# Both feed-forward products by Strassen's algorithm, in a two-block transformer kernel on one core

## The chip, the core and the metric

The kernel runs on one core of a Trainium2 chip. The metric is the device time of one execution in microseconds (us), start to end. The profile calls the engines PE (TensorE, matrix products), PEld (its weight loads), DVE (VectorE), ACT (ScalarE), POOL (GpSimd) and SP (SyncE, which here issues the DMA transfers). SBUF is the on-chip memory; the PE accumulates into PSUM, in banks of 128 x 512 fp32 numbers, which DVE or ACT read out; HBM is the memory off the core.

## What is computed

The input `x` is 1024 x 1024 in fp32. A first block (a pooling mixer and sliding attention) and the attention half of a second block come ahead of the part that matters here, the feed forward at the end. It widens 1024 features to 4096 and brings them back:

```python
def second_block(x, ...):
    ...
    x = x + merged @ w_out
    h2 = rms_norm(x, norm2)
    x = x + jnp.square(jax.nn.relu(h2 @ w_up)) @ w_down    # 1024 -> 4096 -> 1024
    return rms_norm(x, final_norm)
```

## The kernel before, in words

Tiles are 128 partitions x 512 fp32 numbers (256 KB) and come from one pool of slots; a slot is free again when its last reader is done. Nothing is multiplied in fp32 directly: each operand is split into a rounded part `h` and a rest `l = x - h`, and each product of two 128-deep slices is made by three matmuls, h times h, h times l and l times h, into one PSUM bank. ACT makes the `h` (line L106, CAST). The `l` is a subtraction on line L109: weights (`wl`) on POOL, activations (`hl`, `fl`) on DVE. Line L96 holds every matmul, L101 every transpose on the PE, L140 the weight loads by DMA.

The program is written out without hardware loops, and each engine executes its own list in order. An emitter sets that order: `e.at(dt, f)` puts an operation into its engine's list when the PE's emitted work has gone on by `dt` ns, `e.need(key)` forces what a matmul needs into the lists ahead of it, and `interleave(a, b, ...)` mixes two such pieces. These dt only decide the order; waiting is done by semaphores.

The feed forward has eight rounds `c`. Each makes 512 hidden features (function `g_T` with `up_evac`): 4 groups x 2 halves of the rows x 8 slices x 3 = 192 matmuls of 512 columns, result transposed. ACT takes the bank by a relu (L1397), DVE squares (L1399), ACT and DVE split (L106, L109). Then `down(c)` adds that round's part of the second product to the residual, which stays in SBUF: 8 row tiles x 2 halves x 4 slices x 3 = 192 matmuls, each bank added by one DVE operation (L1424). The last round's `down_last` also squares for the final norm (L380) and scales (L1452, L1453); there the last row tile's second half is made in two pieces of 256 columns. All eight rounds hold 3,072 matmuls of 512 columns' worth.

Ahead of it stands `out2(1)`, which ends the attention half: DVE evacuates (L1372), ACT squares and sums (L380), POOL forms the reciprocal root (L114, L115), DVE scales (L1380). The PE transposes the scaled rows (L101, tile `xs` to bank `tp`), ACT and DVE make the split from the bank (L392 `hh`, L396 `hl`). Those transposes are mixed between matmuls, four row tiles in `out2(1)`, the others in the first round.

## Time and profile before

| what | us |
|---|---|
| median of 3 runs (lowest, highest) | 1907.5 (1907.17, 1907.57) |
| the profiled execution's own time | 1907.2 |
| its span, first to last instruction | 1905.5 |
| PE busy in the span | 1881.4 |
| DVE, ACT, POOL busy | 904.5, 792.1, 497.0 |
| feed forward's first matmul; the last matmul's end | 1198.48; 1898.83 |

The profiled execution is 1.7 us longer than its span and 0.3 us below the median. The page of the profile gives busy time by engine and in 40 slices of the span (47.6 us each); a digit is tenths of the slice.

### The profile page before, as it was taken

What the parts mean: (1) busy time and instruction counts of PE and PEld (TensorE: products, weight loads), DVE (VectorE), ACT (ScalarE), POOL (GpSimd) and SP (SyncE); (2) the same over time, 40 slices, a digit from 0 to 9 for tenths busy, and PEclk for the clock granted to TensorE, in tenths of its full rate; (3) what the DMA queues carried; (4) which work ended last, traced back from release to release, by engine and by line L of the source; (5) the groups of instructions that cost most, each with busy time, mean ns of one, the idle gap of its engine ahead of it and who ended that gap; (6) DMA issues with size and microseconds to landing.
All of it is one profiled execution on the core that took longest, in us unless ns stands there. A gap on an engine that the chain in (4) does not pass through costs nothing.

```text
span 1905.5 us, 25049 instructions
## 1 busy us (share of the span) xinstructions
PE 1881.4 (99%) x9401; PEld 1587.8 (83%) x9401; DVE 904.5 (47%) x1841; ACT 792.1 (42%) x1677; POOL 497.0 (26%) x545
## 2 busy tenths in 40 slices
PE   7999999999999999999999999999999999999998
PEld 6888878898898888889888888888888888888887
DVE  6587882735555565665664524422232222222225
ACT  6455463537657676564553222313030212212033
POOL 4122242603312222221112322223140312213131
PEclk9999999999999999999999999999999999999999
DMA  7011132404323222111117341102111111102012
...
DMA packets 152313, 128.51 MB, mean 67 GB/s; under 512 B 12848, under 2 KB 120064, under 8 KB 152192
## 3 DMA queue, kind: packets, MB, share of 16 engines
...
q14 instruction: 47, 0.39, 0.1%
...
## 4 chain that ended last, share of the span: by engine, by line
PE 93%; DVE 3%; ACT 2%; issue 1%; POOL 1%; DMA 0%; POOLq 0%; SPq 0%; ACTq 0%; DVEq 0%
PE mm L96 56%; PE mmo L96 25%; PE tp L101 4%; PE S L96 4%; PE O L96 4%; DVE s L906 1%; ACT junk L380 0%; POOL ry L115 0%; DVE sb L641 0%; ACT sb L632 0%; DVE x L760 0%; DVE ptl L109 0%; DVE sb L626 0%; DMA x<-in_x 0%; ACT q L455 0%
## 5 line engine op out<-in xcount | busy, mean ns | idle before, releaser
L109 POOL TENSOR_TENSOR wl<-wr,wh 128x512 fp32r<-128x512 f32 x292 | 396.5, 1364 | 1104.8 <-ACT wh L106 542.7
L96 PE MATMUL mm<-hh,wh 128*128 128x512 f32 (+1 forms) x1048 | 413.7, 395 | 0.0
L96 PE MATMUL mm<-hl,wh 128*128 128x512 f32 (+1 forms) x1048 | 409.6, 391 | 1.6 <-DVE hl L791 1.6
L96 PE MATMUL mm<-hh,wl 128*128 128x512 f32 (+1 forms) x1048 | 409.0, 390 | 0.0
L96 PEld LDWEIGHTS mm<-hh,wl 128*128 128x128 f32 x1048 | 197.7, 189 | 42.4
L96 PEld LDWEIGHTS mm<-hl,wh 128*128 128x128 f32 x1048 | 198.2, 189 | 36.4 <-DVE hl L791 2.1
L96 PEld LDWEIGHTS mm<-hh,wh 128*128 128x128 f32 x1048 | 198.2, 189 | 35.2
L632 ACT ACTIVATE sb<-sb,nm 128x128 f32<-128x128 f32 (+2 forms) x192 | 125.6, 655 | 149.4 <-DVE nm L626 99.2
L1397 ACT ACTIVATE r<-mmo 128x512 f32<-128x512 f32 x32 | 19.2, 599 | 382.1 <-PE mmo L96 382.1
L106 ACT CAST wh<-wr 128x512 fp32r<-128x512 f32 x292 | 175.7, 616 | 0.7 <-DMA wr<-in_w_in 0.3
L109 DVE TENSOR_TENSOR ptl<-tp,pth 128x512 fp32r<-128x512 f32 (+2 forms) x176 | 113.5, 646 | 79.9 <-ACT pth L106 75.8
L1399 DVE TENSOR_TENSOR r<-r 128x512 f32<-128x512 f32 x64 | 44.3, 692 | 204.8 <-ACT r L1397 204.8
L106 ACT CAST pth<-tp 128x512 fp32r<-128x512 f32 (+2 forms) x176 | 96.4, 548 | 74.0 <-PE tp L101 69.8
L96 PE MATMUL mmo<-hh,wh 128*128 128x512 f32 x272 | 106.9, 393 | 0.0
L96 PE MATMUL mmo<-hh,wl 128*128 128x512 f32 x272 | 105.9, 389 | 0.0
L96 PE MATMUL mmo<-hl,wh 128*128 128x512 f32 x272 | 105.8, 389 | 0.0
L101 PE MATMUL tp<-ident,sb 128*128 128x128 f32 x648 | 99.7, 272 | 1.3 <-DVE ptl L109 1.0
L641 DVE TENSOR_SCALAR sb<-sb,rc 128x128 f32<-128x128 f32 (+2 forms) x192 | 97.6, 508 | 6.7
L96 PE MATMUL mmo<-wh,fh 128*128 128x512 f32 x260 | 100.7, 387 | 0.0
L96 PE MATMUL mmo<-wl,fh 128*128 128x512 f32 x260 | 100.7, 387 | 0.0
L96 PE MATMUL mmo<-wh,fl 128*128 128x512 f32 x260 | 100.7, 387 | 0.0
L101 PEld LDWEIGHTS tp<-ident,sb 128*128 128x128 f32 x648 | 80.5, 140 | 22.9 <-DVE ptl L109 1.8
...
## 6 DMA issues: line engine op xcount, KB each, us to landing
wr<-in_w_in SPq DMA_DIRECT2D x116, 256.0 KB, 3.4
wr<-in_w_up SPq DMA_DIRECT2D x64, 256.0 KB, 3.2
wr<-in_w_down SPq DMA_DIRECT2D x64, 256.0 KB, 3.2
wr<-in_w_out SPq DMA_DIRECT2D x32, 256.0 KB, 3.8
g_d<-g SPq DMA_DIRECT2D x32, 256.0 KB, 2.1
gl<-g_d SPq DMA_DIRECT2D x32, 256.0 KB, 5.8
...
x<-in_x SPq DMA_DIRECT2D x16, 256.0 KB, 2.9
```

The costliest lines, as they stand in the source:

```text
L96: self.nc.tensor.matmul(out=out, lhsT=lhsT, rhs=rhs, start=start, stop=stop)
L101: self.nc.tensor.transpose(out, in_, ident)
L106: self.nc.scalar.copy(out, in_)
L109: (eng or self.nc.vector).tensor_tensor(out=out, in0=in0, in1=hi.bitcast(F32), op=ALU.subtract)
L632: ACT.activation(d[:, 0:w], d[:, 0:w], AF.Exp, bias=nm, scale=-1.0, accum_out=g.sm[:, j:j + 1])
L641: V.tensor_scalar(out=d[:, 0:w], in0=d[:, 0:w], scalar1=g.rc[:, j:j + 1], scalar2=None, op0=ALU.mult)
L906: V.tensor_tensor(out=nxt[:, a0:1040], in0=cur[:, a0:1040], in1=cur[:, a0 - n:1040 - n], op=ALU.add)
L1397: ACT.activation(r0, ps, AF.Relu)
L1399: e.at(600, lambda: V.tensor_tensor(out=r1, in0=r0, in1=r0, op=ALU.mult))
```

## The change

Both products of the feed forward are done by Strassen's algorithm, in Winograd's form (7 products of half-size blocks instead of 8, with 15 sums). In the first product `q` counts 16 pairs of feature groups. Each `q` has 7 products of 4 slices x 3 matmuls = 84 matmuls of 512 columns; the sums over weight blocks (4 for each `q`, line L1491) are made on DVE from loaded tiles, and the sums over blocks of the activations once, from the transposes' banks (`prep0` L1606 to L1608, `prep1` L1625 to L1627, and L1635). Products 1 and 2 accumulate in one bank, and so do 5 and 3; a copy or a sum of the bank is taken in between (L1695, L1743, L1686), and the PE waits for it. The first three `q` go through `up_first` in another product order while the transposes of the second half are mixed in: eight transposes, twelve matmuls, eight transposes, four times. The other thirteen go through `up_pair`, with six PSUM banks in turn.

ACT makes relu and square of a hidden tile (L1660, L1661), DVE four sums of hidden tiles for each `q` (in `sums`), and the seven operands are stored to `hid_d` in HBM, 256 KB each (L1655). The residual goes to HBM too (L1420). The second product has 4 rounds `c` of 7 products x 4 row tiles x 4 slices x 3 = 336 matmuls. Each reads 28 hidden tiles back (L1540) and 16 weight tiles (L1545), makes 16 weight sums (L1491) and 56 splits: `h` on ACT (L109), `l` on POOL or, 5 of 14, on DVE (L112). DVE adds the banks to sums in SBUF (L1686; in round 0 two of the seven products are copied by ACT, L1830), 28 a round. The final norm's last piece is 512 columns wide. The feed forward has 2,688 matmuls of 512 columns. The core of the diff:

```diff
+        if self.wide:
+            pool, tag = ((self.mmp, "mm"), (self.op, "O"), (self.tp, "T"))[self.turn % 3]
+            return pool.tile([128, 512], F32, name="mm" + tag, tag=tag)
...
+    def tick(self):
+        if self.pos < min(self.goal, len(self.steps)) and self.e.t >= self.next:
+            self._one()
+            self.next = self.e.t + self.gap
+    def need(self, key, ahead):
+        i = self.mark[key]
+        while self.pos < i:
+            self._one()
+        self.goal = max(self.goal, i + ahead)
...
-    for c in range(8):
-        for f in range(4):
-            W.add(f"up{c}{f}", colunit(w_up, c * 512 + f * 128))
-        for f in range(4):
-            W.add(f"dn{c}{f}", [rowhalf(w_down, 4 * c + f, ch) for ch in range(2)])
...
+                        SY.dma_start(out=x2_d[t * 128:(t + 1) * 128, 512 * j:512 * j + 512], in_=x2.pop((t, j)))
...
+        def split(self, src, dst, last, on_dve=0):
+
+            def f():
+                r = self.raw.pop(src) if last else self.raw[src]
+                h, l = e.u(F32R, "fh"), e.u(F32R, "fl")
+                e.hi(h, r)
+                self.n_lo += 1
+                eng = V if self.n_lo * on_dve % 14 < on_dve else POOL
+                self.late.append(lambda: e.lo(l, r, h, eng))
+                self.parts[dst] = (h, l)
+            self.step(f, src, mark=dst)
...
+        def comb(self, dst, x, y, op, eng=V):
+            def f():
+                if dst not in self.raw:
+                    self.raw[dst] = e.u(name="cb")
+                eng.tensor_tensor(out=self.raw[dst], in0=self.raw[x], in1=self.raw[y], op=op)
+            self.step(f, x, y)
...
+    ORDER = (1, 2, 7, 6, 4, 5, 3)
...
+        for q in qs:
+            sp(q, "a", 1, 1), sp(q, "w", "11", 1, False)
+        for q in qs:
+            cm(q, "t3", "12", "22"), sp(q, "a", 2, 2), sp(q, "w", "21", 2, False)
+        for q in qs:
+            cm(q, "12", "12", "11"), sp(q, "a", 7, 7), cm(q, "11", "22", "12"), sp(q, "w", "t3", 7)
+        for q in qs:
+            cm(q, "21", "21", "11"), sp(q, "a", 6, 6), sp(q, "w", "11", 6)
+        for i, n in ((4, "21"), (5, "12"), (3, "22")):
+            for q in qs:
+                sp(q, "a", i, i), sp(q, "w", n, i)
...
+            ps = tr4(0, k)
+            key = ("11", k) if k < 4 else ("12", k - 4)
+            r = HR[key] = e.u(name="hr")
+            h, l = HA[key] = e.u(F32R, "hh"), e.u(F32R, "hl")
+            g = gains[:, 2, k:k + 1]
+            e.at(50, lambda ps=ps, h=h, g=g: ACT.activation(h, ps, AF.Copy, scale=g))
+            e.at(650, lambda ps=ps, r=r, g=g: ACT.activation(r, ps, AF.Copy, scale=g))
+            e.at(800, lambda ps=ps, h=h, l=l, g=g: V.scalar_tensor_tensor(
+                out=l, in0=ps, scalar=g, in1=h.bitcast(F32), op0=ALU.mult, op1=SUB), ("A", *key))
+            yield 436.0
...
+            p21, p22 = tr4(1, k), tr4(1, k + 4)
+            e.at(50, lambda p22=p22, h=h, g2=g2: ACT.activation(h, p22, AF.Copy, scale=g2))
+            e.at(50, lambda p21=p21, x21=x21, g1=g1: V.tensor_scalar(out=x21, in0=p21, scalar1=g1, scalar2=None, op0=ALU.mult))
+            e.at(800, lambda p21=p21, s3=s3, g1=g1, r11=r11: stt(s3, p21, g1, r11, SUB))
+            e.at(1500, lambda p22=p22, s1=s1, g2=g2, x21=x21: stt(s1, p22, g2, x21, ADD))
+            e.at(2200, lambda p22=p22, l=l, g2=g2, h=h: stt(l, p22, g2, h.bitcast(F32), SUB), ("A", "22", k))
+            e.at(2900, lambda p22=p22, s2=s2, g2=g2, s3=s3: stt(s2, p22, g2, s3, ADD), ("s2", k))
+            asplit("s1", k, s1, 2400, POOL)
+            asplit("s3", k, s3, 4500, POOL)
+            asplit("s2", k, s2, 5500, V)
+            e.at(12000 + 1000 * k, lambda r12=r12, s2=s2: V.tensor_tensor(out=r12, in0=r12, in1=s2, op=SUB))
+            asplit("s4", k, r12, 14000 + 1000 * k, POOL)
+            yield 872.0
...
+    def prod(ps, q, i, first=True, ahead=11):
+        wh, wl = F.take((q, i), ahead)
+        for k in range(4):
+            e.need(("A", ANAME[i], k))
+            h, l = HA[ANAME[i], k]
+            c = slice(k * 128, k * 128 + 128)
+            e.mm(ps, wh[:, c], h, first and k == 0, False, not first)
+            e.mm(ps, wh[:, c], l, False, False, not first)
+            e.mm(ps, wl[:, c], h, False, k == 3, not first)
+            yield 650.0
...
+    def sums(q):
+        h11, h12, h21, h22 = (hs.pop((q, n)) for n in ("11", "12", "21", "22"))
+        s1, s3 = e.u(name="hc"), e.u(name="hc")
+        V.tensor_tensor(out=s3, in0=h21, in1=h11, op=SUB)
+        V.tensor_tensor(out=s1, in0=h21, in1=h22, op=ADD)
+        store(q, 1, h11), store(q, 4, h22), store(q, 5, s1), store(q, 7, s3)
+        s2 = h21
+
+        def f():
+            V.tensor_tensor(out=s2, in0=h22, in1=s3, op=ADD)
+            s4 = e.u(name="hc")
+            V.tensor_tensor(out=s4, in0=h12, in1=s2, op=SUB)
+            store(q, 2, h12), store(q, 6, s2), store(q, 3, s4)
+        e.at(1800, f)
...
+        for q in qs:
+            ps = e.mmt()
+            yield from prod(ps, q, 1, True, 6)
+            e.at(50, lambda q=q, ps=ps: keep(1, q, ps), ("keep", q))
+            e.need(("keep", q))
+            yield from prod(ps, q, 2, False, 6)
+            e.at(50, lambda q=q, ps=ps: c11(q, ps))
...
+    def up_pair(q):
+        st = {}
+        X = e.mmt()
+        yield from prod(X, q, 1)
+
+        def k1():
+            st["u2"] = e.u(name="pk")
+            ACT.copy(st["u2"], X)
...
+        Y = e.mmt()
+        yield from prod(Y, q, 6)
+        e.need(("k1", q))
+        e.at(50, lambda: vadd(st["u2"], Y, st["u2"]), ("u2", q))
+        yield from prod(X, q, 2, False)
+        e.at(50, lambda: c11(q, X))
+        Z = e.mmt()
+        yield from prod(Z, q, 7)
+
+        def k3():
...
+        Vb = e.mmt()
+        yield from prod(Vb, q, 5)
+
+        def k5():
+            c = e.u(name="hc")
+            vadd(c, Vb, st["u3"])
+            relu2(c, c, q, "22")
+        e.at(50, k5, ("k5", q))
...
+        e.need(("k5", q))
+        yield from prod(Vb, q, 3, False)
...
-            for ch in range(2):
-                ps = e.mmt()
-                yield from n_group(ps, hid, t // 4, t, {f: wp[f][ch] for f in range(4)}, range(4))
-                xt = x2[t, ch]
-                e.at(50, lambda ps=ps, xt=xt: V.tensor_tensor(out=xt, in0=ps, in1=xt, op=ALU.add))
...
+    def down_prod(c, i):
+        qs = range(4 * c, 4 * c + 4)
+        F.s.gap, F.look = 800.0, 14
+        for q in qs:
+            F.s.need((q, "w", i), 14)
+        F.flush()
+        ops = [(F.parts.pop((q, "a", i)), F.parts.pop((q, "w", i))) for q in qs]
+        go_on = i in (2, 3)
+        for t in range(4):
+            tc_ = slice(t * 128, t * 128 + 128)
+            if go_on:
+                e.need(("bank", t))
+            else:
+                banks[t] = e.mmt()
+            ps = banks[t]
+            for j, ((h, l), (wh, wl)) in enumerate(ops):
+                e.mm(ps, h[:, tc_], wh, j == 0 and not go_on, False, go_on)
+                e.mm(ps, h[:, tc_], wl, False, False, go_on)
+                e.mm(ps, l[:, tc_], wh, False, j == 3, go_on)
+                yield 650.0
+            if go_on:
+                del banks[t]
+            if c == 0 and i in (1, 7):
+                g = acc[i, t] = e.u(name="acc")
+                e.at(50, lambda ps=ps, g=g: ACT.copy(g, ps), ("bank", t))
...
+            g = acc[1 if i == 6 else i, t]
+            e.at(50, lambda ps=ps, g=g: vadd(g, ps, g), ("bank", t))
...
+    for c in range(4):
+        for i in ORDER:
+            if c == 0 and i in (2, 4, 5, 3):
+                for t in range(4):
+                    x_load(i, t)
+            run(down_prod(c, i))```

Where instructions stand now shows at three places. First ACT, where the feed forward begins; `junk` is the sum of squares for the norm, `x_...` a row tile. Before, with the relu `r` of the first bank and the splits `hh` of the transposes:

```order
L392 ACTIVATE hh<-tp,gains 128x512 x3
L380 ACTIVATE junk,ss_11798<-x_12001 128x512
L380 ACTIVATE junk,ss_11831<-x_12054 128x512
L392 ACTIVATE hh<-tp,gains 128x512
L1397 ACTIVATE r<-mmo 128x512
L106 CAST fh<-r 128x512
L392 ACTIVATE hh<-tp,gains 128x512 x4
```

Of the change, with the copy `pk` of a bank after product 1 and the relu and square `hc` after product 2:

```order
L407 ACTIVATE junk,ss_11798<-x_11987 128x512
L407 ACTIVATE junk,ss_11827<-x_12053 128x512
L1695 COPY pk<-mmo 128x512
L1660 ACTIVATE hc<-mmo 128x512
L1661 ACTIVATE hc<-hc 128x512
L1626 ACTIVATE hh<-tp,gains 128x512
L1695 COPY pk<-mm 128x512
L109 CAST hh<-hr 128x512
L1626 ACTIVATE hh<-tp,gains 128x512
L109 CAST hh<-hr 128x512
L109 CAST fh<-wr 128x512
L1660 ACTIVATE hc<-mm 128x512
```

The copy is new between the two halves of one accumulation, and splits of sums (`hh<-hr`) have joined. Second DVE, at the same place. Before:

```order
L1380 TENSOR_SCALAR xs<-x_11727,ry 128x512
L1380 TENSOR_SCALAR xs<-x_12054,ry 128x512
L396 SCALAR_TENSOR_TENSOR hl<-tp,gains,hh 128x512
L1399 TENSOR_TENSOR r<-r 128x512
L109 TENSOR_TENSOR fl<-r,fh 128x512
L396 SCALAR_TENSOR_TENSOR hl<-tp,gains,hh 128x512 x4
```

Of the change:

```order
L1415 TENSOR_SCALAR xs<-x_12053,ry 128x512
L1627 TENSOR_SCALAR hr<-tp,gains 128x512
L1625 SCALAR_TENSOR_TENSOR hr<-tp,gains,hr 128x512 x2
L1625 SCALAR_TENSOR_TENSOR hl<-tp,gains,hh 128x512
L1625 SCALAR_TENSOR_TENSOR hr<-tp,gains,hr 128x512
L1627 TENSOR_SCALAR hr<-tp,gains 128x512
L1625 SCALAR_TENSOR_TENSOR hr<-tp,gains,hr 128x512 x2
L1625 SCALAR_TENSOR_TENSOR hl<-tp,gains,hh 128x512
L112 TENSOR_TENSOR hl<-hr,hh 128x512
L1625 SCALAR_TENSOR_TENSOR hr<-tp,gains,hr 128x512
```

For a pair of banks DVE had two operations (`hl`); now it has five, and from the second pair on a split of a sum (L112) among them. Third DVE in the second product, round 1, as product 2 gives way to product 7. Before, this engine's list in `down` held only the additions:

```order
L1424 TENSOR_TENSOR x_11531<-mmo,x_11531 128x512
L1424 TENSOR_TENSOR x_11832<-mm,x_11832 128x512
L1424 TENSOR_TENSOR x_11533<-mmo,x_11533 128x512
L1424 TENSOR_TENSOR x_11834<-mm,x_11834 128x512
L1424 TENSOR_TENSOR x_11547<-mmo,x_11547 128x512
```

Of the change, with the weight sums (`wr<-wr`) and the rests `fl`:

```order
L1686 TENSOR_TENSOR x_15187<-mmT,x_15187 128x512
L1491 TENSOR_TENSOR wr<-wr 128x512 x2
L112 TENSOR_TENSOR fl<-cb,fh 128x512
L1686 TENSOR_TENSOR x_15189<-mmmm,x_15189 128x512
L1491 TENSOR_TENSOR wr<-wr 128x512
L1686 TENSOR_TENSOR x_15191<-mmO,x_15191 128x512
L1491 TENSOR_TENSOR wr<-wr 128x512 x2
L112 TENSOR_TENSOR fl<-ha,fh 128x512
L1491 TENSOR_TENSOR wr<-wr 128x512
L1686 TENSOR_TENSOR x_15193<-mmT,x_15193 128x512
L1491 TENSOR_TENSOR wr<-wr 128x512
L112 TENSOR_TENSOR fl<-wr,fh 128x512
```

Weight sums and rests now stand in one list with the additions that free the banks.

## Rows read from the trace of the kernel before

**Rows 1.** The page of the profile: the span, then each engine's busy us, share and instruction count, then the busy tenths of PE in 40 slices and the TensorE clock that was granted in each.

```profile
span 1905.5 us, 25049 instructions
...
PE 1881.4 (99%) x9401; PEld 1587.8 (83%) x9401; DVE 904.5 (47%) x1841; ACT 792.1 (42%) x1677; POOL 497.0 (26%) x545
...
PE   7999999999999999999999999999999999999998
...
PEclk9999999999999999999999999999999999999999
```

**Rows 2.** Busy time in two stretches, before the feed forward and the feed forward: stretch, its us, then busy us (and instruction count) of PE, PEld, DVE, ACT, POOL, the granted clock, the DMA engines' busy share, GB/s.

```profile
0.00:1198.48 1198.48, 1181.07 (x6286) 1007.50 (x6286) 692.54 (x1548) 627.49 (x1375) 317.90 (x395) 1.00 0.27 78
1198.48:1898.83 700.35, 700.34 (x3117) 580.27 (x3115) 210.64 (x290) 163.36 (x299) 177.99 (x147) 1.00 0.16 50
```

**Rows 3.** The chain of work that ended last, three pieces in the feed forward: start, us, what, and how many instructions.

```profile
1300.27 5.44 PE mmo L96 x24
...
1675.63 5.44 PE mm L96 x24
1681.07 2.72 PE mmo L96 x12
```

**Rows 4.** PE's timeline around one group of four transposes: start, us of one, line, operation. The matmul ahead of the transposes starts at 1205.53.

```profile
1205.53 0.40 PE L96 MATMUL mm<-hh,wl 128*128 128x512 f32 x1
1205.76 0.60 PE L101 MATMUL tp<-ident,xs 128*128 128x128 f32 x4
1206.12 0.47 PE L96 MATMUL mm<-hh,wh 128*128 128x512 f32 x1
1206.43 0.39 PE L96 MATMUL mm<-hl,wh 128*128 128x512 f32 x1
```

**Rows 5.** ACT's timeline: it takes a finished bank, at the point where the first piece of [rows 3] begins.

```profile
1300.30 0.60 ACT L1397 ACTIVATE r<-mm 128x512 f32<-128x512 f32 x1 [2.88 <-PE mm L96]
```

**Rows 6.** ACT's and DVE's timelines at the entry to the feed forward: start, us, operation, idle time before it and what ended it.

```profile
1184.54 0.69 ACT L392 ACTIVATE hh<-tp,gains 128x512 fp32r<-128x512 f32 x1 [1.14 <-PE tp L101]
...
1185.26 0.75 DVE L396 SCALAR_TENSOR_TENSOR hl<-tp,gains,hh 128x512 fp32r<-128x512 f32 x1 [1.07 <-ACT hh L392]
...
1198.68 0.69 DVE L1372 SCALAR_TENSOR_TENSOR x<-mm,x 128x512 f32<-128x512 f32 x1 [1.78 <-PE mm L96]
...
1199.46 0.60 ACT L380 ACTIVATE junk<-x 128x512 f32<-128x512 f32 x1 [4.67 <-DVE x L1372]
```

**Rows 7.** Groups of instructions by line and shape from 1300 to 1800 us: operands, count | busy us, mean ns of one | idle us before them and what ended it.

```profile
L109 POOL TENSOR_TENSOR wl<-wr,wh 128x512 fp32r<-128x512 f32 x94 | 131.1, 1402 | 345.6 <-issue 212.8 <-ACT wh L106 116.4 <-DMA wr<-in_w_up 12.2
L106 ACT CAST wh<-wr 128x512 fp32r<-128x512 f32 x94 | 56.1, 615 | 0.0
L109 DVE TENSOR_TENSOR fl<-r,fh 128x512 fp32r<-128x512 f32 x47 | 42.6, 907 | 34.0 <-ACT fh L106 29.9 <-PE mmo L96 4.1
L1399 DVE TENSOR_TENSOR r<-r 128x512 f32<-128x512 f32 x47 | 32.6, 693 | 156.2 <-ACT r L1397 156.2
L1424 DVE TENSOR_TENSOR x<-mmo,x 128x512 f32<-128x512 f32 x46 | 31.8, 692 | 81.2 <-PE mmo L96 81.1
L1397 ACT ACTIVATE r<-mm 128x512 f32<-128x512 f32 x24 | 14.4, 599 | 73.3 <-PE mm L96 73.3
```

**Rows 8.** Durations of one kind of operation over the whole span, count, then ns shortest/median/longest, first and last start, and shape (first three rows); then four timeline rows of POOL and DVE, two where they overlap in time and two where they don't, start and us.

```profile
L109 POOL TENSOR_TENSOR wl<-wr,wh x292: 1277/1297/1897, 7.9 to 1846.9; 128x512 fp32r<-128x512 f32 x146
...
L109 DVE TENSOR_TENSOR fl<-r,fh x64: 691/962/1026, 1207.3 to 1857.2; 128x512 fp32r<-128x512 f32 x64
...
L1334 DVE TENSOR_TENSOR gl<-gl x16: 691/692/1306, 1027.0 to 1108.6; 128x512 f32<-128x512 f32 x16
...
1301.49 3.00 POOL L109 TENSOR_TENSOR wl<-wr,wh 128x512 fp32r<-128x512 f32 x2 [2.39 <-ACT wh L106]
...
1302.31 1.02 DVE L109 TENSOR_TENSOR fl<-r,fh 128x512 fp32r<-128x512 f32 x1 [0.69 <-ACT fh L106]
...
1329.52 0.69 DVE L109 TENSOR_TENSOR fl<-r,fh 128x512 fp32r<-128x512 f32 x1 [0.69 <-ACT fh L106]
...
1335.52 5.06 POOL L109 TENSOR_TENSOR wl<-wr,wh 128x512 fp32r<-128x512 f32 x4 [9.28 <-ACT wh L106]
```

**Rows 9.** Transfers. First a stretch with the most traffic, for the matmuls alone: stretch, its us, busy us (and count) of PE and PEld, granted clock, DMA share, GB/s; then all packets from 1198 to 1898 us; then DMA issues on SP, start, us of eight, and of one kind the count, KB each and median us from issue to landing, for a store to HBM and the load of the same data.

```profile
1025.00:1047.00 22.00, 22.00 (x99) 18.22 (x98) 1.00 1.07 351
...
DMA packets 40233, 34.82 MB, mean 50 GB/s; under 512 B 2064, under 2 KB 30736, under 8 KB 40198
...
1010.47 3.72 SPq L1281 DMA_DIRECT2D oa<-o_d  x8
...
g_d<-g SPq DMA_DIRECT2D x32, 256.0 KB, 2.1
gl<-g_d SPq DMA_DIRECT2D x32, 256.0 KB, 5.8
```

**Rows 10.** The end: DVE's and ACT's last additions and sums of squares, of 512 and of 256 columns.

```profile
1896.39 0.69 DVE L1438 TENSOR_TENSOR x<-mmo,x 128x512 f32<-128x512 f32 x1
...
1897.17 0.60 ACT L380 ACTIVATE junk<-x 128x512 f32<-128x512 f32 x1 [0.46 <-DVE x L1438]
...
1898.85 0.42 DVE L1438 TENSOR_TENSOR x<-mmo,x 128x256 f32<-128x256 f32 x1 [0.25 <-PE mmo L96]
...
1899.37 0.39 ACT L380 ACTIVATE junk<-x 128x256 f32<-128x256 f32 x1 [0.63 <-DVE x L1438]
```

More of the change, by code (lines that the diff above doesn't have):

```diff
@@ L72, in pe @@
         self.t += ns
-        if self.weights is not None:
-            self.weights.tick()
+        for w in self.streams:
+            w.tick()
         while self.heap and self.heap[0][0] <= self.t:
@@ L1360, in out2 @@
             W.want(0, base + min(5, (t + 1) // 2 + 1), base + min(4 if ch == 0 else 3, (t + 2) // 2))
+            if ch == 1 and t >= 3:
+                F.load(0, min(N0, t - 2))
+                F.ahead(6 * min(N0, t - 3))
             for k in range(8):
@@ L1365, in out2 @@
             out2_evac(ch, t, ps)
+            if t == 3 and ch == 1:
+                for k in range(8):
+                    del mT[k, 0]
     def out2_evac(ch, t, ps):
@@ new lines, in block_kernel, with asplit, tr4 @@
+    for c in range(4):
+        down_steps(c)
+    HA, HR = {}, {}
+    def asplit(key, k, r, dt, eng):
+        h, l = e.u(F32R, "hh"), e.u(F32R, "hl")
+        HA[key, k] = (h, l)
+        e.at(dt, lambda: e.hi(h, r))
+        e.at(dt + 650, lambda: e.lo(l, r, h, eng), ("A", key, k))
+    def tr4(half, k):
+        ps = e.tp.tile([128, 512], F32, name="tp", tag="T")
+        for j in range(4):
+            e.tr(ps[:, j * 128:(j + 1) * 128], xs2[4 * half + j][:, k * 128:(k + 1) * 128], ident)
+        return ps
@@ new lines, in prep0 @@
+    def prep0():
+        for t in range(4):
+            e.need(("xs2", t))
+        for k in range(KT):
+            ps = tr4(0, k)
[9 more added lines that the diff above has]
+        for t in range(4):
+            xs2.pop(t)
@@ L1458, in block_kernel @@
[L1458 to L1475 removed]
+    interleave(up_first(), prep1, lambda: xs2_t[7], 4)
@@ new lines, in gain, with last @@
+    def gain(t, ch):
+        y = e.u(name="xg")
+        V.tensor_tensor(out=y, in0=xgf[t, ch], in1=gfin[:, 512 * ch:512 * ch + 512], op=ALU.mult)
+        xgf[t, ch] = y
+    def last(row, tail=False):
+        ss, x = ssf.pop(row), [xgf.pop((row, ch)) for ch in range(2)]
+        POOL.tensor_tensor(out=ss[:, 2:3], in0=ss[:, 0:1], in1=ss[:, 1:2], op=ADD)
+        r = e.rstd(ss[:, 2:3])
+        for ch in range(2):
+            if not tail:
+                V.scalar_tensor_tensor(out=x[ch], in0=x[ch], scalar=r, in1=gfin[:, 512 * ch:512 * ch + 512],
+                                       op0=ALU.mult, op1=ALU.mult)
+            elif ch == 0:
+                V.tensor_scalar(out=x[ch], in0=x[ch], scalar1=r, scalar2=None, op0=ALU.mult)
+            else:
+                ACT.activation(x[ch], x[ch], AF.Copy, scale=r)
+            SY.dma_start(out=out_d[row * 128:(row + 1) * 128, 512 * ch:512 * ch + 512], in_=x[ch])
@@ L1476, in block_kernel @@
+    for c in range(4):
+        for i in ORDER:
+            if c == 0 and i in (2, 4, 5, 3):
+                for t in range(4):
+                    x_load(i, t)
+            run(down_prod(c, i))
     e.flush()
```

323 lines of the change are left out of this document (246 added, 77 removed).

## The prediction, made before the changed kernel had run

> **What bounds the kernel now.** I began with the page's busy times [rows 1]: PE works 1881.4 of 1905.5 us, every other engine under half, and after the first slice every digit of PE is 9 at the full clock. The two stretches [rows 2] say it more sharply for the part that changes: in the feed forward's 700.35 us PE is busy for 700.34, while DVE has 210.64, ACT 163.36, POOL 177.99. The chain of waits there [rows 3] is matmul after matmul with nothing between: 24 in 5.44 us, so 0.2267 us each. That accounts for the stretch: 3,072 x 0.2267 = 696.3, and eight groups of transposes at some 0.46 (from the matmul at 1205.53 to that at 1206.12 are 0.59 us where 0.23 would do, and the next one comes late by another 0.1 [rows 4]) are 3.7; together 700.0. So the time here is the number of matmuls, as long as the operands arrive.
>
> **The change, part by part.** The sum is made against the profiled execution, 1907.2 us, which is 0.3 below the median.
>
> *Fewer matmuls.* 3,072 become 2,688, each of the same shape: 384 x 0.2267 = 87.0 us less. The number of transposes does not change. This leaves 1820.2, and from there on only waits of PE can be added.
>
> *The three copies in `up_first`.* Product 2 goes on in the bank that ACT copies first, and PE has nothing else in its list. ACT takes a bank at 1300.30, 0.03 us after the next bank's matmuls begin [rows 3, 5], so the drain is short; the copy has the size of that relu, 0.60. With the drain and PE's restart I take 0.85 each, 2.6 in all; between the copy alone (1.8) and 1.3 each when ACT is still in another operation (4).
>
> *The second half's transposes.* A pair of transposed banks was read by two operations of DVE, now by five, and both banks are free only after the last. Each such operation is some 0.66 apart (0.75 for one alone [rows 6]): 3.3 us for a pair, 0.4 for the transposes to land, and from the second pair on 0.7 for the split of a sum that stands between and itself waits for a cast on ACT. That is 4.4 us against what PE has in that time, twelve matmuls (2.72) and eight transposes (0.9): 3.6. So nothing at the first pair, 0.8 at each of the next two, and about 1 more where ACT's cast comes late behind a relu and a square. I take 2.5; 1 to 5 as the ends.
>
> *The first half's transposes* lie in `out2(1)`, where a row tile is 7.3 us of PE: 24 matmuls, 5.44, and four groups of transposes at 0.46. ACT has two operations a group by 0.6, a sum of squares with its readout, 0.7, and some three casts of 0.6 [rows 6, 7]: 7.3 as well. It just fits; a late cast or `hl` would show here. I take 1 us, 0 to 3.
>
> *From three pairs to one.* At the end of `up_first` DVE has fifteen sums that empty the banks and join products, twelve sums of hidden tiles and four of the next weights, 31 x 0.69 = 21.4 us [rows 7], while PE has products 7 and 3 of three pairs, 6 x 2.72 = 16.3. What is left over, 5 us, meets the next pair, whose additions stand behind it in DVE's list, and the stores of 21 tiles wait for the same sums. PE has about 4 us before it needs the first of those additions. So I take 2; 0 where DVE catches up in time, 6 where all of it is waited for.
>
> *The steady first product.* For each pair PE has 84 x 0.2267 = 19.04 us. POOL has 7 rests x 1.30 = 9.1 [rows 8], ACT about 16 operations x 0.6 = 9.7, DVE 13 x 0.69 = 9.0 [rows 7]. A bank comes up again after one product, 2.72 us, against the copy's 0.85. Hidden: 0. If this cover went, rival two has the price.
>
> *The second product.* A round is 336 x 0.2267 = 76.2 us of PE. POOL has 36 rests (46.8), ACT 56 casts (34), DVE 16 weight sums, 20 rests and 28 additions (64 x 0.69 = 44). On average this is hidden. It is not even, though: as the order shows, the sums of the weights fall into products 2 to 6, and there the additions that free PE's banks stand behind sums and rests, which wait for ACT. In product 7 DVE has 8 sums, 3 rests and 4 additions, 10.4 us by 0.69, 10.9 us of PE. Any overlap with POOL, which makes the rest 0.907 and not 0.69 [rows 7], puts DVE over it. I take 1 us a round, 4; between 0 and 3 a round (12).
>
> *The trip through HBM.* The feed forward moved 34.82 MB [rows 9]. Now the weights come to 33.6, the hidden tiles to 29.4 each way (16 x 7 x 262 KB), the residual to 4.2 each way, the output to 4.2: 105 MB in some 627 us, 167 GB/s; round 0 of the second product 206 GB/s. Matmuls at the full clock went on beside 351 GB/s, PE without a gap [rows 9]. SP issues eight in 3.72 us; 400 issues are 190 us. A store landed in 2.1, its load in 5.8 us. The loads are asked for a whole product ahead (10.9 us). Hidden: 0; what else could happen is rival three.
>
> *The tail.* The last piece is 512 columns wide: addition 0.69 for 0.42, squares 0.60 for 0.39 [rows 10], +0.5.
>
> The sum: -87.0 + 2.6 + 2.5 + 1 + 2 + 0 + 4 + 0 + 0.5 = -74.4, so 1907.2 - 74.4 = 1832.8; the 0.3 to the median is below what I can tell. **1833 us.** By the lower ends (1.8, 1, 0, 0, 0) it is 1907.2 - 87.0 + 2.8 + 0.5 = 1823.5, by the upper (4, 5, 3, 6, 12) 1907.2 - 87.0 + 30 + 0.5 = 1850.7.
>
> **DVE against POOL.** POOL's rest takes 1.30 alone and two of them 3.00 in the trace; the DVE rest that runs beside them takes 1.02, where one that has no POOL beside it takes 0.69 [rows 8]. In the worst case in the trace DVE's sum of two tiles took 1.306 and POOL's rest 1.897. So both slow each other, by 0.2 to 0.6 us an encounter. The change brings more such encounters: in a round of the second product 36 DVE operations with two SBUF inputs (24.8 us) beside 36 on POOL (46.8).
>
> The extreme would be that they exclude each other wholly: a round would then need 24.8 + 46.8 = 71.6 of PE's 76.2 us, a pair of the first product 8 x 0.69 + 9.1 = 14.6 of 19.04. That is still below PE on average, but the second product would be left without room for uneven stretches; rival two prices it. The row of the longest sum, 1.306, is 0.69 and half of a POOL operation, so something like it happens at times; the mean of 0.907 says that it is not the habit, and the sum above goes by that.
>
> The Trainium skill has a rule on this, in "SBUF — State Buffer", section "Who interferes with whom": a DVE instruction with two SBUF inputs and a GpSimd instruction that reads SBUF contend for a shared pair of ports, which one holds exclusively, while the other blocks. The trace agrees in that both get longer; that one waits for all of the other, the median rest of 0.962 beside POOL does not show. By the rule the time is that of rival two, 1840 to 1850; by the rows it is 1833.
>
> **The rivals.**
>
> *One: every wait is hidden.* Then only the copies are left: 1907.2 - 87.0 + 0.5 + about 2 = 1821 to 1826. For it: PE waited for nothing in 700 us [rows 2], and its list is emitted well ahead. Against it: twelve matmuls between transposes are less than DVE's chain.
>
> *Two: DVE and POOL, each held up by the other, become the bound in the second product.* With 71.6 us of 76.2, products 7 and 6 wait in each round. For it: by the means [rows 7], in which encounters are contained, 36 x 0.907 + 36 x 1.402 = 83.1, 6.9 us over in each of four rounds: 28 more. Such means count each encounter twice, so I take half of that, 14, in place of the 4: 1843, and 1840 to 1850 around it. Against it: the additions read a bank and one tile, and at 692 ns [rows 7] show no lengthening.
>
> *Three: the slots.* Tiles wait for stores, loads for slots, SP's list is in order, so that a store that waits for a late sum holds up weight loads behind it. If each of the 16 pairs and four rounds loses 1 to 3 us, it is 1850 to 1890. For it: the traffic is three times as much. Against it: 10.9 us of lead against 5.8.
>
> *Four: slower than before.* As in two, but in both products and lasting: were DVE's sums and POOL's rests wholly exclusive and each f times as long as alone, PE would wait 13 x (14.6 f - 19.04) + 4 x (71.6 f - 76.2) us, from the two sums above. This reaches the 74.4 that are won at f = 1.31; with the longest rows (1.306 and 1.897) it would be about 217, some 2045 us. POOL's mean of 1402 is f = 1.08. That the PE's work would not be saved I can exclude, the instructions are counted.
>
> **How the numbers follow.** The forecast, 1826 to 1840: 0.55. Rival one, 1821 to 1826: 0.13. Rival two, 1840 to 1850: 0.17. Rival three: 0.10. Rival four: 0.04, and 0.01 for a gain lost to within 0.2%, 3.8 us, about what a measurement of this kernel can tell from no change. The range 1821 to 1850 holds 0.85 of it; both ends lie where the terms' own bounds do. Faster 0.95, same 0.01, slower 0.04.
>
> **What would show it.** In the changed profile the chain's matmuls should still come at 0.2267 us. PE should idle for some 0.85 us behind ACT's copy L1695 three times; ahead of the second, third and fourth eight transposes behind DVE's L1625; once by a few us where `up_pair` begins; then not at all until the second product, where waits behind DVE or POOL L112 in products 7 and 6 should come to about 1 us a round. The feed forward should move some 170 GB/s with no wait for a DMA. From the last matmul's end to the span's should be 7.2 us, against 1905.5 - 1898.83 = 6.7 [rows 1, 2]. I am wrong if PE waits in every pair of the first product (rival two or four), if loads end PE's waits (three), or if the clock granted leaves full speed.

## The result, and the profile after

The changed kernel takes 1861.07 us (median of 4 runs, 1860.17 to 1861.37) against 1907.34 before: a ratio of 0.9757, interval 0.974 to 0.9774. The forecast had 1833 and a range up to 1850. So the change gains 46 us and not 74, and the time lies outside the range. It falls into the 1850 to 1890 of rival three, but by chance: that rival's waits for transfers are not there, as the waits below show. The profiled execution took 1860.17, its span is 1858.4 us.

The page's first parts, as in [rows 1], here with the digits of DVE and POOL:

```profile
span 1858.4 us, 25772 instructions
...
PE 1803.5 (97%) x9005; PEld 1518.3 (82%) x9005; DVE 1151.9 (62%) x2071; ACT 927.8 (50%) x1926; POOL 711.2 (38%) x684
...
PE   7999999999999999999999999998999999999986
...
DVE  6578783645464556655675541658666568768685
...
POOL 4123242512212212211211231374455558777563
PEclk9999999999999999999999999999999999999988
```

PE is no longer full: slice 28 has an 8, the last two have an 8 and a 6, and in these two the clock falls too. The stretches, in the columns of [rows 2]: the first product, rounds 0 to 2 of the second, round 3, and from PE's last matmul to the end.

```profile
1200.42:1523.44 323.02, 311.64 (x1377) 256.27 (x1376) 205.64 (x235) 161.37 (x286) 171.67 (x127) 0.99 0.46 153
1523.44:1753.20 229.76, 228.78 (x1009) 189.11 (x1008) 173.05 (x191) 103.11 (x188) 171.88 (x113) 1.00 0.54 179
1753.20:1844.82 91.62, 81.57 (x337) 65.81 (x335) 70.22 (x83) 29.16 (x66) 46.66 (x44) 0.93 0.22 74
1844.82:1858.40 13.58, 0.16 (x1) 0.00 (x0) 5.81 (x9) 2.17 (x5) 2.11 (x7) 0.68 0.31 116
```

Rounds 0 to 2 cost 77.44, 76.16 and 76.16 us, 336 x 0.2267 being 76.2: together 1.3 us of waits, less than was forecast. Round 3 costs 15.5 more than 76.2, the tail (the last of the four stretches) 13.6 where it was 6.7 [rows 1, 2]. What PE waited for, from 1190 us to the end (us in total, times, longest):

```profile
PE mmmm L99 <- DVE fl L112: 6.5, 1, 6.5
PE mmO L99 <- ACT pk L1743: 6.0, 1, 6.0
PE mmO L99 <- DVE fl L112: 4.5, 2, 3.5
PE mmo L99 <- ACT pk L1695: 2.3, 2, 1.6
PE tp L104 <- DVE hr L1625: 2.2, 2, 1.8
PE mm L99 <- ACT pk L1695: 0.7, 1, 0.7
PE tp L104 <- DVE hl L1608: 0.3, 1, 0.3
PE mm L99 <- DVE hl L1625: 0.3, 1, 0.3
```

There are no waits on a DMA among them and none inside the thirteen steady pairs once the first of them has got its copy. Three are large: 6.0 where `up_pair` begins (1273 to 1280 us), 6.5 in product 4 of round 3 (1799 to 1806), 3.5 in its last product (1830 to 1834).

**The wait at the first pair.** ACT's and DVE's timelines, start, us, operation, and ACT's idle time:

```profile
1277.38 0.63 ACT L1660 ACTIVATE pk<-pk 128x512 f32<-128x512 f32 x1 [3.17 <-DVE pk L1686]
1278.04 0.63 ACT L1661 ACTIVATE pk<-pk 128x512 f32<-128x512 f32 x1
1278.58 0.60 ACT L109 CAST fh<-wr 128x512 fp32r<-128x512 f32 x1
1279.09 0.58 ACT L1743 COPY pk<-mmO 128x512 f32<-128x512 f32 x1
...
1272.88 1.59 DVE L1678 TENSOR_TENSOR hc<-pk 128x512 f32<-128x512 f32 x1
1274.40 1.75 DVE L1670 TENSOR_TENSOR hc<-pk,hc 128x512 f32<-128x512 f32 x1
1276.07 0.68 DVE L1671 TENSOR_TENSOR hc<-pk,u 128x512 f32<-128x512 f32 x1
1276.67 0.68 DVE L1686 TENSOR_TENSOR pk<-mm,pk 128x512 f32<-128x512 f32 x1
```

The copy that PE waits for stands in ACT's list behind a relu, and this relu waits for an addition that stands in DVE's list behind sums of hidden tiles. Two of these take 1.59 and 1.75 us, not 0.69.

**The wait in round 3.** DVE and POOL side by side:

```profile
1790.76 1.08 DVE L1852 TENSOR_TENSOR x<-x,acc 128x512 f32<-128x512 f32 x1
1791.76 1.77 DVE L1853 TENSOR_TENSOR acc<-acc 128x512 f32<-128x512 f32 x1
1793.57 3.36 DVE L1855 TENSOR_TENSOR x<-x,acc 128x512 f32<-128x512 f32 x2
1796.86 1.77 DVE L112 TENSOR_TENSOR fl<-ha,fh 128x512 fp32r<-128x512 f32 x1
...
1791.26 3.43 POOL L112 TENSOR_TENSOR fl<-wr,fh 128x512 fp32r<-128x512 f32 x2
1794.64 3.44 POOL L112 TENSOR_TENSOR fl<-ha,fh 128x512 fp32r<-128x512 f32 x2
```

Both engines go in step, one operation each in 1.70 us, where DVE alone would need 0.61 and POOL 1.25 from start to start. The four sums of each row tile (L1852 to L1855, sixteen in all, which close Strassen's second product) stand ahead of the rests `fl` that PE waits for. From 1804.8 to 1815.7 POOL is idle, and the same four sums on DVE, for the third row tile, are short again:

```profile
1806.57 0.69 DVE L1852 TENSOR_TENSOR x<-x,acc 128x512 f32<-128x512 f32 x1
1807.18 0.68 DVE L1853 TENSOR_TENSOR acc<-acc 128x512 f32<-128x512 f32 x1
1807.89 1.29 DVE L1855 TENSOR_TENSOR x<-x,acc 128x512 f32<-128x512 f32 x2
```

The rest that ends PE's wait is DVE's at 1805.25. From 1780 to 1815 us DVE has no gap worth naming, so that rest is late by what stands ahead of it in the list and not by a cast. The eight sums and one rest from 1790.76 to 1805.25 take 8 us more than they would at the length that they have beside an idle POOL, which is more than the 6.5 that PE waits (an estimate from the trace's rows).

**The tail.** One row of the last product on three engines:

```profile
1838.32 0.69 DVE L1686 TENSOR_TENSOR x<-mmO,x 128x512 f32<-128x512 f32 x1
1841.04 1.41 DVE L1885 SCALAR_TENSOR_TENSOR x<-x,ry,gf 128x512 f32<-128x512 f32 x2 [2.04 <-POOL ry L118]
1842.37 0.68 DVE L1686 TENSOR_TENSOR x<-mmT,x 128x512 f32<-128x512 f32 x1
...
1839.10 0.60 ACT L407 ACTIVATE junk<-x 128x512 f32<-128x512 f32 x1 [3.33 <-DVE x L1686]
...
1839.90 0.20 POOL L1881 TENSOR_TENSOR ss<-ss 128x1 f32<-128x1 f32 x1 [2.95 <-ACT junk L407]
```

Addition, square on ACT, root on POOL, scaling, and only then the next row's addition: 4.05 us a row, during 2.04 of which DVE waits with the next bank ready. PE delivers a row in 2.72. Eight rows run through this chain.

### The profile page after: what moved, and what is told of

Same layout as the page of the kernel before. It is cut to its first block, busy times and chain, and to the rows that moved or that the text cites. A ratio compares the mean times of both kernels' runs of the same rounds, so it can differ in the third digit from the quotient of the medians.

```text
span 1858.4 us, 25772 instructions
## 1 busy us (share of the span) xinstructions
PE 1803.5 (97%) x9005; PEld 1518.3 (82%) x9005; DVE 1151.9 (62%) x2071; ACT 927.8 (50%) x1926; POOL 711.2 (38%) x684
## 2 busy tenths in 40 slices
PE   7999999999999999999999999998999999999986
DVE  6578783645464556655675541658666568768685
POOL 4123242512212212211211231374455558777563
## 4 chain that ended last, share of the span: by engine, by line
PE 83%; DVE 8%; ACT 3%; issue 3%; POOL 2%; DMA 1%; SPq 0%; POOLq 0%; ACTq 0%; DVEq 0%
PE mm L99 38%; PE mmO L99 9%; PE mmT L99 8%; PE mmmm L99 8%; PE mmo L99 7%; PE tp L104 4%; PE S L99 4%; PE O L99 4%; DVE wr L1491 1%; ACT junk L407 1%; POOL ry L118 1%; DVE s L933 1%; DVE fl L112 1%; POOL fl L112 0%; ACT fh L109 0%
## 5 line engine op out<-in xcount | busy, mean ns | idle before, releaser
L112 POOL TENSOR_TENSOR wl<-wr,wh 128x512 fp32r<-128x512 f32 x164 | 219.0, 1341 | 619.1 <-ACT wh L109 381.9
L99 PE MATMUL mm<-hh,wh 128*128 128x512 f32 (+1 forms) x792 | 313.7, 396 | 0.0
L99 PE MATMUL mm<-hl,wh 128*128 128x512 f32 (+1 forms) x792 | 309.9, 391 | 1.3 <-DVE hl L818 1.3
L99 PE MATMUL mm<-hh,wl 128*128 128x512 f32 (+1 forms) x792 | 309.2, 390 | 0.0
L112 POOL TENSOR_TENSOR fl<-wr,fh 128x512 fp32r<-128x512 f32 x148 | 214.6, 1464 | 104.8 <-ACT fh L109 91.2
L99 PEld LDWEIGHTS mm<-hh,wl 128*128 128x128 f32 x792 | 149.6, 189 | 32.5
L99 PEld LDWEIGHTS mm<-hl,wh 128*128 128x128 f32 x792 | 150.1, 189 | 26.3 <-DVE hl L818 1.8
L99 PEld LDWEIGHTS mm<-hh,wh 128*128 128x128 f32 x792 | 150.0, 189 | 25.3
L112 DVE TENSOR_TENSOR ptl<-tp,pth 128x512 fp32r<-128x512 f32 (+2 forms) x176 | 113.5, 646 | 79.9 <-ACT pth L109 75.9
L112 POOL TENSOR_TENSOR fl<-ha,fh 128x512 fp32r<-128x512 f32 x80 | 124.0, 1564 | 68.8 <-ACT fh L109 28.5
L109 ACT CAST fh<-wr 128x512 fp32r<-128x512 f32 x192 | 115.7, 615 | 39.2 <-DVE wr L1491 23.9
L109 ACT CAST pth<-tp 128x512 fp32r<-128x512 f32 (+2 forms) x176 | 96.4, 548 | 74.0 <-PE tp L104 69.8
L109 ACT CAST fh<-ha 128x512 fp32r<-128x512 f32 x112 | 69.2, 618 | 70.5 <-PE mmO L99 20.5
L1491 DVE TENSOR_TENSOR wr<-wr 128x512 f32<-128x512 f32 x96 | 101.5, 1061 | 2.4 <-POOL fl L112 0.7
L104 PE MATMUL tp<-ident,sb 128*128 128x128 f32 x648 | 99.7, 272 | 1.2 <-DVE ptl L112 0.9
L407 ACT ACTIVATE junk<-x 128x512 f32<-128x512 f32 (+1 forms) x53 | 34.1, 644 | 131.3 <-DVE x L1686 68.8
L109 ACT CAST wh<-wr 128x512 fp32r<-128x512 f32 x164 | 99.2, 616 | 0.9 <-DMA wr<-in_w_in 0.5
L104 PEld LDWEIGHTS tp<-ident,sb 128*128 128x128 f32 x648 | 80.5, 140 | 22.9 <-DVE ptl L112 1.8
L99 PE MATMUL O<-pth,v 128*128 128x256 f32 (+3 forms) x264 | 93.2, 361 | 0.0
L99 PE MATMUL S<-kh,q 128*128 128x256 f32 (+3 forms) x264 | 79.7, 315 | 2.8 <-DVE nm L653 2.8
## 6 DMA issues: line engine op xcount, KB each, us to landing
wr<-in_w_in SPq DMA_DIRECT2D x116, 256.0 KB, 3.4
ha<-hid_d SPq DMA_DIRECT2D x112, 256.0 KB, 3.8
hid_d<-hc SPq DMA_DIRECT2D x77, 256.0 KB, 2.7
wr<-in_w_up SPq DMA_DIRECT2D x64, 256.0 KB, 4.7
wr<-in_w_down SPq DMA_DIRECT2D x64, 256.0 KB, 5.2
wr<-in_w_out SPq DMA_DIRECT2D x32, 256.0 KB, 4.1
x_d<-x SPq DMA_DIRECT2D x32, 256.0 KB, 2.2
g_d<-g SPq DMA_DIRECT2D x32, 256.0 KB, 2.1
```

The lines of the kernel that those rows point to most:

```text
L99: self.nc.tensor.matmul(out=out, lhsT=lhsT, rhs=rhs, start=start, stop=stop, skip_group_check=skip)
L104: self.nc.tensor.transpose(out, in_, ident)
L109: self.nc.scalar.copy(out, in_)
L112: (eng or self.nc.vector).tensor_tensor(out=out, in0=in0, in1=hi.bitcast(F32), op=ALU.subtract)
L407: ACT.activation(j[:, 0:n], src, AF.Square, accum_out=acc)
L1491: eng.tensor_tensor(out=self.raw[dst], in0=self.raw[x], in1=self.raw[y], op=op)
```

## The experiments

Four accounts of the three losses stood against each other: A, the order and crowding of DVE's list in the last round; B, DVE and POOL shutting each other out; C, slots and transfers on the way through HBM; D, DVE's pile of sums at the end of `up_first`. Most runs are the changed kernel with one edit; `two`, `best` and `best2` join several, and `down_only` takes the first product back. The kernel before took 1907.1 to 1907.2 us beside them.

**The order of the last round's list.** `late_scale` moves one thing, the scaling behind the next row's addition:

```diff
-        for ch in range(2):
-            if not tail:
-                V.scalar_tensor_tensor(out=x[ch], ...)
+        if not tail:
+            def scale(): ...
+            e.at(1700, scale)
+            return
```

> Only the final scaling of a row (two DVE operations, L1885) is put behind the next row's addition in DVE's list. Theory A (in the last round DVE's list is a chain: addition, square on ACT, root on POOL, scaling, and only then the next addition, 4.06 us a row where PE gives a row in 2.72): the 3.5 us that PE waits in product 3 go, and the stretch from PE's last matmul to the end falls from 13.6 us to 7 to 9; 1849 to 1853 us. Rival B (the loss in the last round is DVE and POOL holding each other up): POOL has only single-column operations there, nothing changes; 1860 to 1862 us.

1849.71 us, 11.4 faster than the change. The wait in the last product is gone, and the tail is 8.36 us:

```profile
1839.54:1847.90 8.36, 0.16 (x1) 0.00 (x0) 3.29 (x6) 1.44 (x3) 2.36 (x5) 0.70 0.46 176
```

Theory A holds, and at this place the order of one list cost 11 us.

`spread_sums` takes the sixteen sums apart:

```diff
-                V.tensor_tensor(out=acc[3, t], ...)    # and acc[7], acc[4], acc[5], all at product 6
+                V.tensor_tensor(out=d, in0=d, in1=acc[1, t], op=ADD)
...
+            e.at(100, lambda: V.tensor_tensor(out=acc[4, t], ...))    # at product 4
+            e.at(100, lambda: V.tensor_tensor(out=acc[5, t], ...))    # at product 5, acc[3] too
```

> Only the sixteen sums of the last round (four for each row tile at product 6) are spread over products 6, 4 and 5, one or two a row. Theory A (sixteen sums in one place of DVE's list stand ahead of the rests that product 4 needs): PE's wait of 6.5 us ahead of product 4 falls under 1 us, with it the stretch at the lower clock behind it (2 to 3 us); 1851 to 1854 us. Rival B (the rests are late since POOL itself is full, 100% busy from 1780 to 1805): PE still waits 3 us or more there, for POOL; 1856 to 1861 us.

1857.07 us: the time is in B's range, the mechanism is neither's. The wait in product 4 is gone, as A said, but the last product waits longer, 8.3 and not 3.5 us, and for DVE, not for POOL (PE's waits from 1760 us on):

```profile
PE mmO L99 <- DVE fl L112: 8.3, 1, 8.3
```

The sums had been taken out of one crowd and put into the chain of rows. With both edits (`two`) that should not count any more.

> The late scaling and the spread sums together. Theory A (in the last round DVE's one list is short of time twice, at the sixteen sums and in the chain of rows; spread sums alone moved the wait into the chain): both waits of PE are gone, 6.5 at product 4 and 3.5 at product 3, with their stretches at the lower clock, and the tail is that of the late scaling alone; 1840 to 1843 us. Rival B (the rests are late because POOL and DVE shut each other out there, whoever stands first): a wait of 3 us or more stays ahead of product 4 or 5; 1845 to 1849 us.

1845.25 us, just inside B's range, yet not by B's mechanism: nothing is left in product 4 or 5. A's time is missed too, since 2.5 us are left in the last product and the tail is 9.7 us, not the 8.4 of `late_scale`. The profiled execution also had 7.0 us at the first pair, not 6.0: there one weight sum ahead of the pile took 5.50 us beside POOL's rests, and 1.76 in the change.

**DVE against POOL.** `pool_memset` and `memset_up` take what POOL reads away, in the second and in the first product:

```diff
-                self.late.append(lambda: e.lo(l, r, h, eng))
+                if on_dve and eng is POOL:       # memset_up: if not on_dve
+                    self.late.append(lambda: POOL.memset(l.bitcast(F32), 0.0))
...
```

> In the second product POOL's 144 rests (subtractions that read two tiles) are replaced by a fill with zeros of the same tile, which reads nothing; so the rests' part of these products is left out. Theory B (DVE operations with two tiles in SBUF and POOL operations that read SBUF shut each other out): DVE's weight sums in the second product fall from a mean of 1.06 us to 0.69, the sums of the last round from 1.7 to 0.69, and PE's wait ahead of product 4 from 6.5 to under 2 us; the tail stays; 1850 to 1854 us. Rival (DVE's operations are as long for another reason, their number alone makes the wait): durations stay above 1 us and the time at 1859 to 1861 us.

> In the first product POOL's 112 rests are replaced by a fill with zeros of the same tile; the rests' part of the weights is left out there. Theory B (POOL and two-tile operations of DVE shut each other out): DVE's sums in the first product fall to 0.69 us each, the pile at the first pair is some 5 to 6 us shorter, and the wait of 6.0 us falls to 0 to 2; the steady pairs, which wait for nothing, stay; 1852 to 1856 us. Rival (the pile is a matter of the number of sums): the wait stays at 4 us or more; 1858 to 1862 us.

1849.93 and 1852.01 us: 11.1 and 9.1 faster than the change. DVE's weight sums in the second product, count, ns shortest/median/longest, in the change and then without POOL's reads:

```profile
L1491 DVE TENSOR_TENSOR wr<-wr x48: 674/1178/1792, 1533.6 to 1785.5; 128x512 f32<-128x512 f32 x48
```

```profile
L1494 DVE TENSOR_TENSOR wr<-wr x48: 680/684/693, 1531.5 to 1780.7; 128x512 f32<-128x512 f32 x48
```

The longest falls from 1792 to 693. The waits at product 4 (with `pool_memset`) and at the first pair (with `memset_up`) are gone altogether; with `pool_memset` the tail stays, 13.9 us. Two more things come with this edit: a fill takes POOL 0.53 us, not 1.3, and it doesn't wait for ACT's cast, so the rests are ready sooner as well. That POOL's rests are what lengthens DVE's operations rests on the durations, here and in round 3 of the change, where the sums are short whenever POOL is idle; how much of the 11 and 9 us comes from the readier rests isn't separated.

`all_pool` moves DVE's share of the rests to POOL: `F.split(..., last, 0)` for `5`.

> All 56 rests of a round of the second product go to POOL (5 of 14 were on DVE). Theory B (an operation of DVE with two tiles in SBUF and one of POOL shut each other out, and POOL's part of that is 1.0 of its 1.3 us): a round needs at least 56 x 1.3 = 73 us of POOL alone and some 80 with 16 weight sums between, against PE's 76.2, so every round waits some 5 us or more and the last one, with its sixteen sums, more still; 1875 to 1910 us. Rival A (DVE's list alone is short of time, POOL has room): DVE loses 20 operations a round, the wait ahead of product 4 goes; 1852 to 1856 us.

1876.57 us, 15.5 slower than the change and within B's range, but not by the steady limit that B named: rounds 0 to 2 cost 79.2, 83.6 and 76.2 us, round 3 96.6 where the change needs 91.6. Round 2 gave POOL all its rests and waited for nothing. PE's waits from 1750 us on are now for POOL:

```profile
PE mmO L99 <- POOL fl L112: 12.8, 3, 9.5
PE mmmm L99 <- POOL fl L112: 1.5, 1, 1.5
PE mmT L99 <- POOL fl L112: 0.6, 1, 0.6
```

The 9.5 is in the last product: the rest stands in POOL's list behind the roots of several rows. Round 1's loss is another one, a wait of 5.3 us for one of DVE's additions. Ahead of it in DVE's list stands a single weight sum, while POOL makes sixteen rests on end (first and last of them shown, and that wait):

```profile
PE mmO L99 <- DVE x L1686: 5.3, 1, 5.3
...
1593.90 20.29 DVE L1491 TENSOR_TENSOR cb<-wr 128x512 f32<-128x512 f32 x1
1614.12 0.68 DVE L1686 TENSOR_TENSOR x<-mmO,x 128x512 f32<-128x512 f32 x1
...
1593.76 1.29 POOL L112 TENSOR_TENSOR fl<-wr,fh 128x512 fp32r<-128x512 f32 x1
...
1612.39 1.25 POOL L112 TENSOR_TENSOR fl<-ha,fh 128x512 fp32r<-128x512 f32 x1
```

The sum began 0.14 us behind a rest, ended 0.55 us after the last of them, and took 20.29 us; POOL's rests kept their 1.25 to 1.29. So at times DVE gets no turn at all until POOL pauses. Why the two alternated in round 3 of the change and not here, no run shows. DVE's share of the rests wasn't the fault; what stood beside and ahead of it was.

**Slots and HBM.** `rows` takes two tiles of `up_pair` from another pool (`e.row(...)` for `e.u(...)`), `store_twice` stores every hidden tile to a second place as well.

> Only the two intermediate tiles of each pair in up_pair are taken from another pool, which is idle there, so that the common pool has four more slots. Theory C (the 6.0 us wait at the first pair is for slots: a cast ahead of the copy waits until a store has landed and freed its slot): that wait falls under 2 us and its lower clock (about 2 us) with it; 1853 to 1857 us. Rival D (the wait is DVE's pile of sums at the end of up_first, slots or not): it stays at 4 us or more; 1859 to 1862 us.

> Each of the 112 hidden tiles is stored twice, to two places in HBM: 29.4 MB more, and each slot is held for one transfer longer. Theory: the way through HBM is hidden with room to spare, nothing moves by more than 2 us; 1859 to 1863 us. Rival C (slots or transfers are near their limit): waits for slots grow with it; 1866 us or more.

`rows`: 1860.33 us, the 6.0 us wait is there unchanged. But its first freed slot comes only with the copy that waits, so it says little on slots at that place. `store_twice`: 1861.25 us, 29.4 MB more and no change in the time, with 5.9 us at the first pair (the last product waits 5.0, not 3.5). The way through HBM has room.

`late_hid` puts off the sums of hidden tiles of the first three pairs, and by that the giving back of their slots:

```diff
-                e.at(1500, lambda: sums(q))
+                e.at(1500 + (7000 * q + 2500 if q < N0 else 0), lambda: sums(q))
```

> Only the sums of hidden tiles of the first three pairs are put off, by 2.5, 9.5 and 16.5 us, behind the additions that the next pair waits for; the tiles keep their slots longer. Theory D (the 6.0 us wait at the first copy of up_pair is DVE's pile of sums: a relu that waits for one of them stands ahead of the copy in ACT's list): the wait falls to under 1.5 us, and the stretch at the lower clock behind it goes; 1852 to 1855 us. Rival C (it is a wait for slots that stores give back): the slots come back later, so the wait stays at 6 us or grows; 1861 to 1868 us.

1858.21 us, 2.9 faster, less than D said. The wait fell from 6.0 to 2.7, with slots held longer: rival C is out. What is left of it is ACT's own list (relus, squares and casts without a gap). Some of the gain was given back in the last product, which waited 4.4 and not 3.5.

**One product alone.** `down_only` makes the first product as before and the second by Strassen.

> Only the second product by Strassen; the first is made as in the kernel before, its tiles are summed and stored as in the change. 192 matmuls fewer than before, 43.5 us, which is 1863.7 from the profiled 1907.2. Theory A (the losses of the last round and the tail belong to the second product alone): the waits of 6.5 and 3.5 us, the lower clock behind them and a tail 7 us longer are all there, about 21 us; 1882 to 1888 us. Rival C (they come from the load of both products together, slots and transfers in flight): at most a third of it; 1864 to 1872 us.

1885.33 us, as A said. No wait up to 1750 us, then the same two:

```profile
PE mmT L99 <- DVE fl L112: 6.5, 1, 6.5
PE mmmm L99 <- DVE fl L112: 3.9, 1, 3.9
```

The second product alone thus gains 21.8 us of its 43.5, and its loss doesn't depend on the first.

**Together.** `best` is `two` with `late_hid`; `best2` has the rests of the last two products of round 3 on POOL besides.

> Late scaling, spread sums and late sums of hidden tiles together. If the three losses (the last round's sums, its chain of rows, DVE's pile at the first pair) are separate, the gains add: 11 from the scaling, 8 from the sums, 7 to 8 from the hidden tiles; 1833 to 1836 us. If they share one limit, less than two thirds of that: 1841 us or more.

> As the three rearrangements together, and the rests of the last two products of the last round all on POOL, which has been idle there. Theory A (the remaining wait of 2.4 us ahead of the last product is a rest standing in DVE's list behind sums and scalings): it goes; 1837 to 1839.5 us. Rival: POOL's rest comes as late, since ACT's cast ahead of it is late; 1841 to 1843 us.

`best`: 1841.44 us (ratio 0.9657, interval 0.9642 to 0.9671), 19.6 faster than the change and the fastest here; less than the sum of the forecasts (26 to 27), and the time falls into the range given for one shared limit, though it is three quarters of that sum and not under two thirds. What is missing is seen, since 3.7 us stay at the first pair, 2.4 in the last product, and the tail is 9.7. Its round 3 costs 79.2 us where the change needs 91.6:

```profile
1751.21:1830.37 79.16, 76.77 (x337) 62.72 (x335) 70.84 (x85) 29.68 (x67) 51.71 (x44) 1.00 0.25 83
```

`best2`: 1846.61 us, slower than `best`, against both forecasts. PE waits 7.3 us for POOL in the last product. Its timeline there:

```profile
1821.68 0.42 POOL L1882 TENSOR_TENSOR ss<-ss 128x1 f32<-128x1 f32 x1 [1.81 <-ACT junk L407]
1822.19 0.57 POOL L117 TENSOR_SCALAR ry<-ss 128x1 f32<-128x1 f32 x1
1822.84 0.55 POOL L118 TENSOR_TENSOR ry<-ry,mhalf 128x1 f32<-128x1 f32 x1
1823.36 1.80 POOL L112 TENSOR_TENSOR fl<-wr,fh 128x512 fp32r<-128x512 f32 x1
```

The rest now stands in POOL's list behind the root of a row, which waits for ACT's square, that for DVE's addition, and that for an earlier scaling: the chain of rows again, through another engine's list.

## Why the prediction was wrong, term by term

The terms against the profiled execution of 1907.2, in us:

| term | forecast | measured |
|---|---|---|
| 384 matmuls fewer | -87.0 | -87.0: 12 in 2.72 as before |
| first half's transposes | 1 | 1.9: the feed forward starts at 1200.42, not 1198.48 |
| three copies in `up_first` | 2.6 | 3.4: gaps of 1.97, 1.07 and 1.07 where 0.23 would do |
| second half's transposes | 2.5 | 2.9 |
| from three pairs to one | 2 | 8.4: 6.15 of wait, the rest the clock after it and small gaps |
| steady pairs | 0 | 0 |
| rounds 0 to 2 | 3 | 1.3 |
| round 3 | 1 | 15.5 |
| tail | 0.5 | 6.9 |
| sum | -74.4 | -46.7, so 1860.5 against 1860.17 |

The count of matmuls was right, the second half's transposes to 0.4 us, and HBM was hidden as forecast. Three terms failed; *From three pairs to one* and the rounds together (1.3 + 15.5) passed even their upper ends, 6 and 12, and the tail had none.

*Round 3.* "I take 1 us a round" took the last round for one like the others. The count of DVE's operations left out what the last round has alone: sixteen sums, sixteen scalings. Round 3 then had 16 + 20 + 28 + 16 + 16 = 96 operations, 66 us of 76 by 0.69 and far more beside POOL. `spread_sums`, `two` and `pool_memset` each make the wait in product 4 vanish, so it takes both the sums and POOL's reads to bring it about.

*The tail.* "+0.5" compared the last piece's width. It didn't follow the list: the scaling of a row, which waits for ACT and POOL, stood ahead of the next addition. In the kernel before the same round trip lay in 5.44 us a row. `late_scale` shows what this order cost, 11.4 with the wait in the last product.

*From three pairs to one.* The pile was rightly named, but reckoned at 0.69 a sum. From 1252 to 1277 us eight operations with both inputs in SBUF took 1.36 to 1.79 each, 7.7 us in all more than at 0.68. `memset_up` removes the wait whole; `late_hid` more than half of it by order alone.

The mis-sized thing behind two of the three is the price of DVE beside POOL. I put the mean of 0.907 and the row of 1.02 [rows 7, 8] above a full exclusion and gave rival two 0.17. In that trace POOL was busy a quarter of the time, so the mean showed how seldom they met, and not what a meeting costs. The row [rows 8] was misread as well: when DVE's rest began at 1302.31, POOL's, begun at 1301.49, had only 0.48 of its 1.30 left, and DVE took 0.33 longer (1.02 for 0.69). That is nearly all that there was to wait for, so the row fits the exclusion that the prediction put behind. Now the median weight sum takes 1178 ns, the longest 1792, and in step one of each in 1.70 us, against 0.61 + 1.25 = 1.86 by wholly separate turns. The additions from a bank, with one input in SBUF, stay at 0.69 throughout. This is what the Trainium skill states in "SBUF — State Buffer", section "Who interferes with whom": an instruction of DVE with two SBUF inputs contends with GpSimd reads, one with at most one SBUF input does not. The trace agrees nearly to the full, all but 0.16 of 1.86 us. A crowd of such sums beside POOL's rests should have been priced at the 1.7 us a sum that the steps show, and not at 0.69. Even so rival two, as I put it, was wrong on the place: it expected a wait in each round, and rounds 0 to 2 had 1.3 us between them. The averages held; it was the two crowds that paid. Its time, 1840 to 1850, was too short as well.

Behind each long wait PE also ran at the lower of its two levels (1.2 of 2.4 GHz) for a few us: the granted clock was 0.70 from 1280 to 1285 us, a mean of both levels, and 0.50, the lower one, from 1805 to 1810, with matmuls 0.43 apart there. Behind the three long waits this comes to 1.6, 2.9 and 1.7 us, 6.2 in all (the excess over 0.2267 us of the matmuls 0.3 to 0.6 apart). My sum priced waits without it; that the clock leaves full speed was among its own signs of being wrong, and the only one of them that came.
